# Half of a block product by seven multiplications instead of eight, in a full matmul stream

## The chip, the cores and the metric

One core of a Trainium2 chip. The metric is device microseconds of one execution: the median of three runs of the kernel before is 2508.51 us (2507.36 to 2508.7). The profile is of one more execution, of 2515.92 us, whose span from the first to the last instruction is 2513.9 us.

## The reference

One layer of a hybrid decoder on x of 2048 tokens by 1024 channels, all in float32:

```
h     = rms_norm(x)
proj  = h @ w_in                         # 1024 -> 8716 columns, split into
        u_a, z_a, q, k, v, z_b, xbc, dt, z_c, gate_logits (3 x 1024)
y_a   = s5_mixer(u_a) * silu(z_a)        # diagonal state space model, 512 wide
y_b   = attention(q, k, v) * silu(z_b)   # three dilated windows
y_c   = ssd_mixer(conv(xbc), dt, z_c)    # chunks of 128 tokens, gated norm
g     = sigmoid(gate_logits)
out   = x + (g0*(y_a@proj_a) + g1*(y_b@proj_b) + g2*(y_c@proj_c)) @ w_out
```

## The kernel before

Every product of two float32 matrices is three matmuls: both operands are split into a high part (float32r, written by ACT) and a low part (the rest, by DVE), and hi*hi, lo*hi and hi*lo are summed in PSUM. `ch_unit` (L384 to L394) does that for an output tile of 128 channels by 512 tokens: 8 steps of the contraction (k) by 3, so 24 matmuls of 512 columns.

The input projection takes the tokens in two halves of two blocks of 512 (`tb`). In the first half the columns come in the order q, k, v, z_b, dt and z_c, xbc (with its convolution), u and z, gates; in the second u and z come first. For the gates (`main_gates`, L555) twelve weight tiles of 256 columns come in one after the other, each as one load of 1 MB (`wload`, L353) into the one buffer `wr`, split in four pieces into `wh` and `wl` (L368, L369; six buffers each), and serve four output tiles, which ACT turns into tanh (L571) and SP stores to `g_d`.

A generator yields after each output tile (a unit). Beside the units runs background work: `run` (in `main`) gives it a number of steps between two units. In the first half these are the S5 tables and attention (units 41 to 80), then `ssd(0)` (83 to 135), `a0_early` (86 to 122: norm and transposes of the second half's rows of x, kept in DRAM as `hT_d`) and `out_weights` (88 to 134: the last stage's weights split in hi and lo, kept in DRAM as `pw_d` and `wo_d`). In the second half it is `s5` (153 to 180), `s5_glu` (181 to 196), attention and the start of `ssd(1)`.

A scheduler then lists the instructions of every engine in one fixed order, by its own model of when each becomes ready, and each engine runs its list in that order. SP issues all DMAs. PSUM has three banks for output tiles (`mm`) and five for the background (`c`).

Of the kernel before, what the change touches and what calls it, by code (L numbers as in the profile page):

```python
# [19 lines left out]
S = 2048  # L20
# [10 lines left out]
S5END = 196  # L31
# [118 lines left out]
class Hybrid:  # L150
# [4 lines left out]
    def setup(self, ctx):  # L155
# [29 lines left out]
        self.tab_d = dram("tab_d", [P, 8, 4 * TABW])  # L185
# [6 lines left out]
        self.wo_d = dram("wo_d", [4, P, 2, 8, 256])  # L192

# [57 lines left out]
    def ct(self, name, shape, dt=F32, tag=None, bufs=1):  # L251

        return self.jp.tile(list(shape), dt, name=name, tag=tag or name, bufs=bufs)

# [90 lines left out]

    def wload(self, name, specs):
# [57 lines left out]
    def main_qkv(self, half):  # L404
# [3 lines left out]
        for kind, g in units:  # L408
# [3 lines left out]
            for tb in (2 * half, 2 * half + 1):  # L412
                for pr in range(2):
# [11 lines left out]
                    nc.sync.dma_start(self.out_rows(dst, tb, pr), e)  # L425
# [21 lines left out]
    def main_uz(self, half):  # L447
        nc = self.nc
        for u in range(4):
            wt = self.wtile(f"uz{u}_{half}", [(u * 256, 256)])  # L450
            for tb in (2 * half, 2 * half + 1):
                for m in range(2):
# [16 lines left out]
                    nc.sync.dma_start(dst[r0:r0 + P, :, tb * 64:(tb + 1) * 64], e)  # L469
# [21 lines left out]
    def conv(self, ct, tb, ps):  # L491
# [3 lines left out]
        xb = self.gp.tile([P, 515], F32, name=f"xb_{nm}", tag="xb", bufs=3)  # L495
# [30 lines left out]
        nc.sync.dma_start(d[t0:t0 + 512, c0:c0 + P].rearrange("(i p) c -> p i c", p=P), yt)  # L526

    def main_dtz(self, half):
# [13 lines left out]
        for u in range(1, 3):  # L542
            wt = self.wtile(f"zc{u}_{half}", [(C_ZC + u * 256, 256)])
            for tb in (2 * half, 2 * half + 1):
                for pr in range(2):
# [6 lines left out]
                    nc.sync.dma_start(self.out_rows(self.zc_d, tb, pr)[:, :, u * 256:(u + 1) * 256], e)  # L552
                    yield

    def main_gates(self, half):  # L555
        nc = self.nc
        for u in range(12):
# [4 lines left out]
            for i, (m, tb) in enumerate(order):  # L562
                nm = f"g{u}_{m}_{tb}"
                if u == 11 and i == 2 and half == 0:
                    self.a0_late(2)
                elif u == 11 and i == 2:
                    self.ysplit = [self.load_y(0)]
# [126 lines left out]
    def merge(self):  # L694

        nc = self.nc
        for tt in range(16):
            rows = slice(tt * P, (tt + 1) * P)
            o = self.mp.tile([P, 3, 4, 66], F32, name=f"mo{tt}", tag="mo", bufs=2)
            for g in range(3):  # L700
                nc.sync.dma_start(o[:, g], self.o_d[g][rows])
            zb = self.mp.tile([P, 4, 64], F32, name=f"mz{tt}", tag="mz", bufs=1)
            nc.sync.dma_start(zb, self.zb_d[rows].rearrange("t (h d) -> t h d", d=64))
            sc = self.mp.tile([P, 3, 3, 4], F32, name=f"msc{tt}", tag="msc", bufs=2)
            w, wl, mx, den = sc[:, 0], sc[:, 1], sc[:, 2, 0, :], sc[:, 2, 1, :]
            nc.vector.tensor_max(mx, o[:, 0, :, 65], o[:, 1, :, 65])
            nc.vector.tensor_max(mx, mx, o[:, 2, :, 65])
            nc.vector.tensor_sub(w, o[:, :, :, 65], mx.unsqueeze(1).to_broadcast([P, 3, 4]))
            nc.scalar.activation(w, w, AF.Exp)
            nc.vector.tensor_mul(wl, w, o[:, :, :, 64])  # L710
# [4 lines left out]
            y = self.mp.tile([P, 4, 64], F32, name=f"my{tt}", tag="my", bufs=1)  # L715
            t = self.mp.tile([P, 4, 64], F32, name=f"mt{tt}", tag="mt", bufs=1)
            for g in range(3):
                wb = w[:, g].unsqueeze(2).to_broadcast([P, 4, 64])
                nc.vector.tensor_mul(t if g else y, o[:, g, :, 0:64], wb)
                if g:  # L720
                    nc.vector.tensor_add(y, y, t)
# [4 lines left out]
            yt = self.mp.tile([P, 2, P], F32, name=f"myt{tt}", tag="myt", bufs=1)  # L726
# [40 lines left out]
    def ssd(self, half):  # L767
        nc = self.nc
        for ch in range(half * 8, half * 8 + 8):
            yield from self.ssd_chunk(ch, slice((ch % 8) * 12, (ch % 8) * 12 + 12))  # L770

    def ssd_chunk(self, ch, hs):
# [703 lines left out]
```

## Time and profile before

| | before |
|---|---|
| median of three runs | 2508.51 us |
| profiled execution | 2515.92 us, span 2513.9 us |
| granted TensorE clock, mean | 0.989 |
| PE busy | 2450.5 us (97%) |
| DVE / ACT / POOL busy | 1325.0 / 782.5 / 700.4 us |
| HBM read / written | 304.80 / 145.97 MB |

The page puts 6% of the chain that ended last on each of the three matmul lines of the gates (`ps_g`, L392 to L394). A matmul's busy time runs from its start to its modelled end, and neighbours overlap; how fast a stream goes is read from one start to the next.

### The profile page before, as it was taken

How to read it: one execution, taken by the hardware profiler on the slowest of the kernel's cores; microseconds unless marked ns; L12 is line 12 of the kernel's file. 1: busy time of each engine (PE TensorE's matmuls, PEld its weight loads, DVE VectorE, ACT ScalarE, POOL GpSimd, SP SyncE). 2: the span in 40 equal slices, each digit the busy share in tenths (PEclk: the TensorE clock that was granted, in tenths of full speed). 3: DMA queues.
4: the chain of work that ended last, by engine and by line, in shares of the span. 5: the costliest groups of instructions: out<-in, count | busy, mean ns of one | idle time of the engine just before them, and what ended most of it. 6: DMA issues, size and time to landing. Idle time of an engine off the chain costs nothing.

```text
span 2513.9 us, 40157 instructions
## 1 busy us (share of the span) xinstructions
PE 2450.5 (97%) x15216; PEld 2155.8 (86%) x15216; DVE 1325.0 (53%) x2852; ACT 782.5 (31%) x1656; POOL 700.4 (28%) x737
## 2 busy tenths in 40 slices
PE   8999999999999999999999999999999899999999
PEld 8999988778888888899999988888888678888988
DVE  6963667853544333277765545632334767563321
ACT  4222235443443324222244244533332312121100
POOL 2262243501434430054342000000111455432120
PEclk8999999999999999999999999999999999999999
DMA  6443344447995336455554432433333688887986
GB/s 162 117 147 117 127 134 132 139 135 213 324 340 183 127 100 212 125 160 172 155 171 153 127 107 85 151 122 126 112 126 113 227 294 298 302 293 261 315 291 217
DMA packets 417088, 453.41 MB, mean 180 GB/s; under 512 B 103040, under 2 KB 358272, under 8 KB 409728
## 3 DMA queue, kind: packets, MB, share of 16 engines
q1 hardware_dynamic: 416896, 450.86, 56.2%
q8 instruction: 120, 1.97, 0.3%
q14 instruction: 72, 0.59, 0.1%
HBM read 304.80 MB, written 145.97 MB: 179 GB/s over the span
## 4 chain that ended last, share of the span: by engine, by line
PE 76%; DMA 8%; DVE 8%; POOL 4%; SPq 2%; issue 1%; ACT 1%; DVEq 0%; ACTq 0%; POOLq 0%
PE ps_g L392 6%; PE ps_g L394 6%; PE ps_g L393 6%; PE fp L1299 3%; PE fp L1301 3%; PE fp L1300 3%; PE ao L688 3%; PE ps_xbc L393 2%; PE ps_xbc L394 2%; PE ps_xbc L392 2%; PE ps_uz L394 2%; PE ps_uz L392 2%; PE ps_uz L393 2%; PE op L1332 2%; PE op L1330 2%; PE op L1331 2%
## 5 line engine op out<-in xcount | busy, mean ns | idle before, releaser
L392 PE MATMUL ps_g<-hT_hi,wh_g 128*128 128x512 f32 x768 | 308.4, 402 | 0.6 <-DVE e_uz L466 0.6
L394 PE MATMUL ps_g<-hT_hi,wl_g 128*128 128x512 f32 x768 | 306.4, 399 | 0.0
L393 PE MATMUL ps_g<-hT_lo,wh_g 128*128 128x512 f32 x768 | 305.7, 398 | 0.0
L813 POOL TENSOR_TENSOR sr<-tle,ahl 128x384 fp32r<-128x384 f32 x128 | 119.9, 960 | 447.3 <-PE sd L818 343.2
L392 PEld LDWEIGHTS ps_g<-hT_hi,wh_g 128*128 128x128 f32 x768 | 144.3, 188 | 33.3 <-DVE e_uz L466 1.3
L394 PEld LDWEIGHTS ps_g<-hT_hi,wl_g 128*128 128x128 f32 x768 | 144.5, 188 | 32.8
L393 PEld LDWEIGHTS ps_g<-hT_lo,wh_g 128*128 128x128 f32 x768 | 144.4, 188 | 32.4
L1299 PE MATMUL fp<-fy_hi,fp 128*128 128x512 f32 x384 | 153.9, 401 | 1.8 <-DMA fp<-pw_d 1.3
L1332 PE MATMUL op<-fo,fm_lo 128*128 128x256 f32 x512 | 146.6, 288 | 7.2 <-DVE fm_lo L1312 7.2
L1330 PE MATMUL op<-fo,fm_hi 128*128 128x256 f32 x512 | 148.0, 289 | 4.0 <-DMA fo<-wo_d 2.8
L1301 PE MATMUL fp<-fy_hi,fp 128*128 128x512 f32 x384 | 150.9, 393 | 0.0
L1300 PE MATMUL fp<-fy_lo,fp 128*128 128x512 f32 x384 | 150.3, 391 | 0.0
L1331 PE MATMUL op<-fo,fm_hi 128*128 128x256 f32 x512 | 146.3, 286 | 0.0
L1304 POOL TENSOR_TENSOR fm<-fm,fg 128x512 f32<-128x512 f32 x64 | 85.0, 1328 | 204.4 <-DVE fg L1302 193.7
L667 ACT ACTIVATE sm<-sm,ml 128x256 f32<-128x256 f32 (+1 forms) x192 | 86.4, 451 | 154.4 <-DVE ml L665 127.0
L392 PE MATMUL ps_xbc<-hT_hi,wh_xbc 128*128 128x512 f32 x320 | 129.7, 405 | 0.0
L394 PE MATMUL ps_xbc<-hT_hi,wl_xbc 128*128 128x512 f32 x320 | 129.4, 404 | 0.0
L393 PE MATMUL ps_xbc<-hT_lo,wh_xbc 128*128 128x512 f32 x320 | 129.1, 404 | 0.0
L369 DVE TENSOR_TENSOR wl_g<-wr_g,wh_g 128x512 fp32r<-128x512 f32 x96 | 75.1, 804 | 98.5 <-ACT wh_g L368 93.5
L506 DVE SCALAR_TENSOR_TENSOR ac_cv<-xb_cv,convw,ac_cv 128x512 f32<-128x512 f32 x120 | 101.3, 844 | 38.8 <-ACT ac_cv L504 38.5
L381 PE MATMUL ps_q<-wh_q,hT_hi 128*128 128x256 f32 x384 | 112.2, 293 | 2.1 <-ACT hT_hi L324 1.7
L382 PE MATMUL ps_q<-wl_q,hT_hi 128*128 128x256 f32 x384 | 110.8, 289 | 3.4 <-DVE wl_q L369 3.4
(418 smaller groups left out, 6922.7 us busy)
## 6 DMA issues: line engine op xcount, KB each, us to landing
fp<-pw_d SPq DMA_DIRECT2D x32, 1536.0 KB, 6.9
fo<-wo_d SPq DMA_DIRECT2D x16, 2048.0 KB, 8.7
wr_g<-in_w_in_dram SPq DMA_DIRECT2D x24, 1024.0 KB, 5.4
g_d<-e_g SPq DMA_DIRECT2D x96, 256.0 KB, 2.7
fg<-g_d SPq DMA_DIRECT2D x96, 256.0 KB, 7.4
pw_d<-owh SPq DMA_DIRECT2D x24, 512.0 KB, 7.1
wr_xbc<-in_w_in_dram SPq DMA_DIRECT2D x10, 1024.0 KB, 5.5
x<-in_x_dram SPq DMA_DIRECT2D x32, 256.0 KB, 5.4
```

The lines of the kernel that those rows point to most:

```text
L381: nc.tensor.matmul(ps, hi[:, t], wh, start=kt == 0, stop=False)
L382: nc.tensor.matmul(ps, hi[:, t], wl, start=False, stop=False)
L392: nc.tensor.matmul(ps, wh, hi, start=kt == 0, stop=False)
L393: nc.tensor.matmul(ps, wh, lo, start=False, stop=False)
L394: nc.tensor.matmul(ps, wl, hi, start=False, stop=kt == KT - 1)
L813: nc.gpsimd.tensor_mul(r, self.tle.unsqueeze(1).to_broadcast([P, 3, P]), ahl[:, i, h0:h0 + 3].unsqueeze(2).to_broadcast([P, 3, P]))
L1299: nc.tensor.matmul(ps, W[k][0], yh[k], start=k == k0, stop=False)
L1300: nc.tensor.matmul(ps, W[k][0], yl[k], start=False, stop=False)
L1301: nc.tensor.matmul(ps, W[k][1], yh[k], start=False, stop=k == k1 - 1)
L1330: nc.tensor.matmul(ps, mh[k][:, t], W[k][0], start=k == 0, stop=False)
L1331: nc.tensor.matmul(ps, mh[k][:, t], W[k][1], start=False, stop=False)
L1332: nc.tensor.matmul(ps, mlo[k][:, t], W[k][0], start=False, stop=k == 7)
```

## The change

The gates of the first half are one product of a 3072 x 1024 by a 1024 x 1024 matrix. The changed kernel does it per weight tile as a 2 x 2 block product after Strassen (in Winograd's form): seven products instead of eight, each of 12 matmuls (4 steps of k by 3). Blocks of h are t0 and t1 (the two token blocks) by the two halves of k. The names: products 1 to 7; `S` 1 to 4 are sums of blocks of h, made once; `gt` 1 to 4 are differences of the weight blocks `gr`, made per tile; `gx`, `gz`, `gq` hold copies of partial results.

```diff
+    def sums(self, half):
...
+            for nm, (hi, lo) in (("11", t0[k]), ("12", t0[4 + k]), ("21", t1[k]), ("22", t1[4 + k])):
+                a[nm] = self.ev(f"a{nm}_{half}_{k}")
+                v.tensor_add(a[nm], hi.bitcast(F32), lo.bitcast(F32))
...
+            v.tensor_add(s1, a["21"], a["22"])
+            v.tensor_sub(s2, s1, a["11"])
+            v.tensor_sub(s3, a["11"], a["21"])
+            v.tensor_sub(s4, a["12"], s2)
+            nc.sync.dma_start(self.sum_d[0, k], s2)
+            nc.sync.dma_start(self.sum_d[1, k], s4)
+            for i, x in ((1, s1), (3, s3)):
+                self.split(x, S[i][0][:, k, :], S[i][1][:, k, :])
...
+        hi = self.wp.tile([P, KT, 268], F32R, name=f"S2_{half}_hi", tag="wr", bufs=1)
...
+    def gate_ops(self, u):
...
+        b11, b12, b22, b21 = raw(0, 0), raw(0, 1), raw(1, 1), raw(1, 0)
+        yield put(1, b11)
+        t1 = diff(1, b12, b11)
+        yield put(5, t1)
+        t2 = diff(2, b22, t1)
+        yield put(6, t2)
+        yield put(3, b22)
+        t3 = diff(3, b22, b12)
+        yield put(2, b21)
+        t4 = diff(4, b21, t2)
+        yield put(7, t3)
+        yield put(4, t4)
...
+            for k, (hi, lo) in enumerate(opnd[p]):
+                wh, wl = w[0][:, k, :], w[1][:, k, :]
+                nc.tensor.matmul(ps, wh, hi, start=k == 0 and p in (1, 2, 5), stop=False, skip_group_check=True)
+                nc.tensor.matmul(ps, wh, lo, start=False, stop=False, skip_group_check=True)
+                nc.tensor.matmul(ps, wl, hi, start=False, stop=k == 3 and p in (2, 3, 4), skip_group_check=True)
+            if p == 1:
+                keep(u, f"x{u % 2}", ps)
+            elif p == 5:
+                keep(u, f"z{u % 2}", ps)
+            elif p == 6:
+                keep(u, "q", ps)
+            elif p == 4:
+                d = self.ev(f"g21_{nm}")
+                put(u, 1, 0, ps, d)
+            else:
+                d, b, m = {3: (e.get("q"), 0, 1), 2: (e.get(f"x{u % 2}"), 0, 0), 7: (e.get(f"z{u % 2}"), 1, 1)}[p]
+                nc.vector.tensor_add(d, d, ps)
+                put(u, b, m, d, d)
```

`put` of the products splits a weight block (ACT high, DVE low); `keep` is an ACT copy from PSUM; the last `put` is tanh and store. The second half's gates stay as they were. To make room in SBUF and on the engines, other work moves:

```diff
-        run([(self.s5_setup(), 18, 2, 38)], 40)
+        ssd0, early0 = self.ssd(0), self.a0_early()
+        run([(self.s5_setup(), 18, 2, 38), (early(early0, 5), 5, 20, 40)], 40)
...
-        run([(chain(self.attention(0, 0), self.attention(1, 0)), 40, 41, 80), (self.s5_tables(), 40, 41, 80),
-             (self.ssd_dt(0, self.jp), 3, 73, 80)], 82)
+        run([(chain(self.attention(0, 0), self.attention(1, 0)), 40, 41, 79), (early(tabs, 54), 54, 41, 80),
+             (self.ssd_dt(0, self.jp), 3, 73, 79), (early0, 3, 40, 52)], 80)
...
-        run([(ssd0, 64, 83, 135), (early0, 8, 86, 122), (self.out_weights(), 20, 88, 134)], 136)
+        sums = self.sums(0)
+        run([(tabs, 10, 80, 86), (early(sums, 4), 4, 81, 85)], 85)
+        run([(tabs, 10, 80, 86), (sums, 5, 85, 88)], 88)
...
+        run([(ssd0, 65, 89, 135)], 136)
...
-        run([(self.s5(), 42, 153, 180)], 180)
+        run([(self.s5(), 42, 153, 180), (early(ow, 13), 13, 138, 180)], 180)
...
-        run([(self.s5_glu(), 25, 181, S5END)], S5END)
+        run([(self.s5_glu(), 25, 181, 196), (ow, 7, 180, 196), (self.ssd_dt(1, self.jp), 2, 196, 198)], S5END)
```

The S5 tables come in 16 pieces of half the size instead of 8; `out_weights` in 40 pieces of 512 columns instead of 20 of 1024, with one buffer each; the first half's ssd has two buffers of `sr` and `smm` instead of four and three, one of `sb`, `sbt`, `sct` and `sz` instead of two, and loads its next chunk a step earlier; `merge` is rewritten for smaller tiles; `main_uz` loads its next weight tile a unit after the last instead of at its own start.

On DVE, at the last u and z units and the first gates, the order before is (`e_uz` the last u and z tiles, `sm` and `sx` ssd, `owh` the weight split, `wl_g` the low part of gate weights):

```order
L466 SCALAR_TENSOR_TENSOR e_uz_0_1_7229<-t_uz_0_1_7230,ps_uz_0_1_7204 128x64x8
L821 TENSOR_TENSOR sm_9_7241<-sm_9_7241,sgm_7023 128x384
L466 SCALAR_TENSOR_TENSOR e_uz_1_1_7280<-t_uz_1_1_7281,ps_uz_1_1_7255 128x64x8
L1240 SCALAR_TENSOR_TENSOR owh_8272<-ow_8270,snw,owh_8272 128x1024
L369 TENSOR_TENSOR wl_g_0_0_7553<-wr_g_0_7550,wh_g_0_0_7552 128x2x256
L369 TENSOR_TENSOR wl_g_0_1_7557<-wr_g_0_7550,wh_g_0_1_7556 128x2x256
```

Before, the low parts of the first gate tile stand ahead of these rows and those of the second right behind them. Now the same place reads (`S_0_lo` low parts of the sums of h, `sl` the sums read back from DRAM, `gt` and `wl_g` the operands of products 5 and 6 of the first tile):

```order
L483 SCALAR_TENSOR_TENSOR e_uz_1_0_7646<-t_uz_1_0_7647,ps_uz_1_0_7621 128x64x8
L616 TENSOR_TENSOR S_0_lo<-a_0_3_7567,S_0_hi 128x512
L616 TENSOR_TENSOR S_0_lo<-sl_0_0_7652,S_0_hi 128x512
L999 TENSOR_TENSOR sgm_7836<-sg_7833,tle 128x256
L616 TENSOR_TENSOR S_0_lo<-sl_0_1_7656,S_0_hi 128x512
L483 SCALAR_TENSOR_TENSOR e_uz_0_1_7693<-t_uz_0_1_7694,ps_uz_0_1_7668 128x64x8
L1018 TENSOR_TENSOR sm_0_7892<-sm_0_7892,sgm_7836 128x384
L616 TENSOR_TENSOR S_0_lo<-sl_0_2_7660,S_0_hi 128x512
L616 TENSOR_TENSOR S_0_lo<-sl_0_3_7664,S_0_hi 128x512
L483 SCALAR_TENSOR_TENSOR e_uz_1_1_7723<-t_uz_1_1_7724,ps_uz_1_1_7698 128x64x8
L642 TENSOR_TENSOR gt_1_7744<-gr_01_7734,gr_00_7732 128x512
L616 TENSOR_TENSOR wl_g_5_7747<-gt_1_7744,wh_g_5_7746 128x512
```

The sums of h stand between the last u and z tiles, and the first tile's operands from product 5 on come behind the last `e_uz`. On SP, where the second half's first weight tile is loaded (`wr_uz`), the order before is (`xl` the second half's h read back, `yc_d` an ssd result):

```order
L353 DMA wr_g_0_9825<-in_w_in_dram 128x8x256
L572 DMA g_d<-e_g_1_1_9601 128x512
L860 DMA yc_d<-sz_9294 128x6x128
L572 DMA g_d<-e_g_0_0_9667 128x512
L572 DMA g_d<-e_g_0_1_9712 128x512
L572 DMA g_d<-e_g_1_0_9767 128x512
L353 DMA wr_uz_1_10066<-in_w_in_dram 128x8x256
L572 DMA g_d<-e_g_1_1_9812 128x512
L572 DMA g_d<-e_g_0_0_9868 128x512
```

And now (`gr` raw weight blocks, `gq`, `gx`, `gz`, `g` finished gate tiles):

```order
L637 DMA gr_11_10097<-in_w_in_dram 128x4x128
L697 DMA g_d<-g_g_0_10078 128x512
L637 DMA gr_10_10099<-in_w_in_dram 128x4x128
L697 DMA g_d<-gq_0_10117 128x512
L697 DMA g_d<-gx_0_9789 128x512
L697 DMA g_d<-gz_0_10058 128x512
L973 DMA sct_10020<-cmT_d 128x2x128
L969 DMA sb_10016<-bm_d 128x256
L367 DMA wr_uz_1_10492<-in_w_in_dram 128x8x256
L348 DMA xl_0_10354<-hT_d 128x512
L697 DMA g_d<-g_g_0_10331 128x512
```

The load now has six of the first half's gate stores behind it, before it had five. Its buffer `wr` now holds the high part of sum 2 until product 6 of the last tile; before, it was free as soon as the last gate tile was split.

## Rows read from the trace of the kernel before

**Rows 1.** The page: span; busy us, share, count by engine.

```profile
span 2513.9 us, 40157 instructions
PE 2450.5 (97%) x15216; PEld 2155.8 (86%) x15216; DVE 1325.0 (53%) x2852; ACT 782.5 (31%) x1656; POOL 700.4 (28%) x737
```

**Rows 2.** Busy time by stretch: engines, granted clock, DMA share, rate.

```profile
core 0: us, PE busy (x) PEld busy (x) DVE busy (x) ACT busy (x) POOL busy (x), PEclk, DMA share, GB/s
0.00:200.00 200.00, 186.92 (x1472) 184.26 (x1473) 146.47 (x557) 66.61 (x129) 81.52 (x96) 0.94 0.52 142
585.00:760.00 175.00, 174.36 (x832) 143.47 (x832) 87.38 (x107) 73.52 (x128) 65.25 (x66) 1.00 1.02 321
639.70:972.20 332.50, 331.86 (x1590) 272.45 (x1589) 144.07 (x190) 118.09 (x229) 127.15 (x137) 1.00 0.64 206
1061.00:1200.00 139.00, 133.51 (x1015) 129.26 (x1013) 103.11 (x195) 35.69 (x69) 67.01 (x91) 1.00 0.58 167
1061.00:1420.00 359.00, 345.32 (x2719) 337.20 (x2718) 238.77 (x395) 116.82 (x209) 128.65 (x150) 1.00 0.53 156
1989.40:1996.20 6.80, 4.90 (x14) 3.72 (x15) 6.74 (x14) 0.74 (x3) 1.23 (x3) 0.50 1.05 439
```

**Rows 3.** Timeline of PE among the gates, twenty matmuls apart: start, length.

```profile
703.13 0.39 PE L394 MATMUL ps_g<-hT_hi,wl_g 128*128 128x512 f32 x1
...
707.76 0.40 PE L393 MATMUL ps_g<-hT_lo,wh_g 128*128 128x512 f32 x1
```

**Rows 4.** DVE groups in the gates: count | busy us, mean ns | idle before.

```profile
L369 DVE TENSOR_TENSOR wl_g<-wr_g,wh_g 128x512 fp32r<-128x512 f32 x44 | 38.9, 905 | 30.0 <-ACT wh_g L368 29.9
...
L1240 DVE SCALAR_TENSOR_TENSOR owh<-ow,owh 128x1024 fp32r<-128x1024 f32 x8 | 10.1, 1258 | 12.8 <-ACT owh L1239 12.8
L1240 DVE SCALAR_TENSOR_TENSOR owh<-ow,snw,owh 128x1024 fp32r<-128x1024 f32 x6 | 8.4, 1393 | 7.0 <-ACT owh L1239 7.0
...
L289 DVE TENSOR_SCALAR x<-x,xs 128x512 f32<-128x512 f32 x16 | 7.1, 484 | 7.6 <-POOL xs L246 7.6
```

**Rows 5.** POOL groups of the same stretch, 639.7 to 972.2 us.

```profile
L813 POOL TENSOR_TENSOR sr<-tle,ahl 128x384 fp32r<-128x384 f32 x54 | 49.6, 941 | 104.8 <-PE sd L818 104.8
...
L795 POOL TENSOR_TENSOR sx<-sx,hpar 128x768 f32<-128x768 f32 x7 | 13.8, 1965 | 0.4
...
L797 POOL TENSOR_TENSOR sxdd<-sxd,edc 128x768 f32<-128x768 f32 x7 | 11.5, 1637 | 0.0
L794 POOL TENSOR_TENSOR sxd<-sx,dt 128x768 f32<-128x768 f32 x7 | 10.3, 1474 | 25.7 <-PE syd L827 25.7
```

**Rows 6.** Single DVE and ACT instructions by tile: ns least, median, most.

```profile
L369 DVE TENSOR_TENSOR wl_g<-wr_g,wh_g x96: 675/692/1850, 628.4 to 1957.2; 128x512 fp32r<-128x512 f32 x96
...
L466 DVE SCALAR_TENSOR_TENSOR e_uz<-t_uz,ps_uz x16: 1047/1082/1096, 601.1 to 1062.0; 128x512 f32<-128x512 f32 x16
...
L721 DVE TENSOR_TENSOR my<-my,mt x32: 411/425/1411, 1931.0 to 2254.2; 128x256 f32<-128x256 f32 x32
...
L1082 DVE SCALAR_TENSOR_TENSOR s5ks<-ident,s5dd,s5ks x32: 216/217/223, 274.9 to 566.0; 16x16 f32<-16x16 f32 x32
...
L821 DVE TENSOR_TENSOR sm<-sm,sgm x64: 539/1074/1643, 610.5 to 2288.7; 128x384 f32<-128x384 f32 x64
...
L368 ACT CAST wh_g<-wr_g x96: 603/620/666, 627.7 to 1955.9; 128x512 fp32r<-128x512 f32 x96
...
L465 ACT ACTIVATE t_uz<-ps_uz x16: 587/598/632, 600.3 to 1061.4; 128x512 f32<-128x512 f32 x16
```

**Rows 7.** Waits of PE, 1061 to 1420: waiter, releaser, total, times, longest.

```profile
PE s5yp L1166 <- POOL s5r L1163: 6.8, 6, 2.1
```

**Rows 8.** Waits of PE from 1980 to 2000.

```profile
PE syd L827 <- DVE sm L821: 6.4, 2, 5.8
```

**Rows 9.** DMA issues by line: count, size, median us to landing.

```profile
wr_g<-in_w_in_dram SPq DMA_DIRECT2D x24, 1024.0 KB, 5.4
...
wr_uz<-in_w_in_dram SPq DMA_DIRECT2D x8, 1024.0 KB, 6.1
```

More of the change, by code (lines that the diff above doesn't have):

```diff
@@ L30 @@
 ATTEND = 256
-S5END = 196
+S5END = 198
 class Small:
@@ L253, in ct, with tct @@
         return self.jp.tile(list(shape), dt, name=name, tag=tag or name, bufs=bufs)
+    def tct(self, name, shape, dt=F32, tag=None, bufs=1):
+        return self.tp.tile(list(shape), dt, name=name, tag=tag or name, bufs=bufs)
     def sct(self, name, shape, dt=F32, tag=None, bufs=1):
@@ L448, in main_uz, with weights @@
         nc = self.nc
+        def weights(u):
+            return self.wtile(f"uz{u}_{half}", [(u * 256, 256)]) if u < 4 else None
+        nxt = weights(0)
         for u in range(4):
-            wt = self.wtile(f"uz{u}_{half}", [(u * 256, 256)])
+            wt, nxt = nxt, None
             for tb in (2 * half, 2 * half + 1):
@@ new lines, in split, with load_sum, pinned, raw @@
+    def split(self, x, hi, lo):
+        self.nc.scalar.copy(hi, x)
+        self.nc.vector.tensor_sub(lo, x, hi.bitcast(F32))
+    def load_sum(self, half, i, k, hi, lo):
+        e = self.ev(f"sl{half}_{i}_{k}")
+        self.nc.sync.dma_start(e, self.sum_d[i, k])
+        self.split(e, hi, lo)
+    def pinned(self, out, in_):
+        with self.tc.issue_after(self.anchor):
+            self.nc.sync.dma_start(out, in_)
+    def gate_ops(self, u):
+        nc = self.nc
+        w = self.A["w_in"][0].rearrange("(k p) c -> p k c", p=P)
+        def raw(i, j):
+            t = self.gp.tile([P, 528], F32, name=f"gr{u}_{i}{j}", tag="xb", bufs=3)
+            t = t[:, 0:512].rearrange("p (k c) -> p k c", c=P)
+            c0 = C_G + u * 256 + j * P
+            nc.sync.dma_start(t, w[:, i * 4:i * 4 + 4, c0:c0 + P])
+            return t
+        def diff(i, a, b):
+            t = self.ev(f"gt{u}_{i}", (P, 4, P))
+            nc.vector.tensor_sub(t, a, b)
+            return t
+        def put(p, x):
+            hl = []
+            for y in ("wh", "wl"):
+                t = self.wp.tile([P, 2, 268], F32R, name=f"{y}_g{u}_{p}", tag=y, bufs=6)
+                hl.append(t.rearrange("p k c -> p (k c)")[:, 0:512].rearrange("p (k c) -> p k c", c=P))
+            self.split(x, *hl)
+            return hl
+        b11, b12, b22, b21 = raw(0, 0), raw(0, 1), raw(1, 1), raw(1, 0)
[10 more added lines that the diff above has]
+        yield put(4, t4)
@@ L556, in main_gates, with main_gates_plain @@
+    def main_gates_plain(self, half):
         nc = self.nc
@@ L1418, in main @@
         st, self.jp = open_pool("jp3")
-        ssd, merge = chain(self.ssd_dt(1, self.sp), self.ssd(1)), self.merge()
+        ssd, merge = self.ssd(1), self.merge()
         run([(chain(self.attention(0, 1), self.attention(1, 1), self.attention(2, 1)), 72, S5END + 2, ATTEND),
-             (early(ssd, 12), 12, 236, ATTEND)], ATTEND)
+             (early(ssd, 11), 11, 236, ATTEND)], ATTEND)
         st.close()
```

282 lines of the change are left out of this document (187 added, 95 removed).

## The prediction

> **What bounds the kernel now.** I read the page first. PE is busy for 97% of the span [rows 1], but neighbouring matmuls overlap in that count, so the reader should go on to the table of stretches: from 639.7 to 972.2 us, where the first half's gates run, PE is idle for 0.6 of 332.5 us at a full clock (1.00, 2.4 GHz), while DVE works 144.1 and POOL 127.2 us [rows 2]. There the kernel is bound by the number of matmuls. It isn't everywhere: from 0 to 200 us PE lacks 13.1 us with DVE busy for 146.5, and from 1061 to 1200 it lacks 5.5 of 139 us with DVE busy for 103.1, 74% [rows 2]. So two questions decide. What does a matmul cost in the full stream, and does the added work push DVE into the state in which PE waits?
>
> **What is removed.** In the timeline, twenty gate matmuls start between 703.13 and 707.76 us [rows 3]: 4.63 / 20 = 0.2315 us each, well under the 0.39 us that one is shown as busy. Before, the first half's gates are 12 tiles x 4 units x 24 = 1152 matmuls; now 12 x 7 products x 12 = 1008 of the same shape. 144 x 0.2315 = 33.3 us go, and since PE has no gaps there, all of it is on the path. The transposes of `a0_early` only move.
>
> **The seam into the gates.** Product 1 uses blocks that exist, product 5 needs all of sum 1 and weights made after the last u and z unit. On DVE, 60 instructions stand between the first `e_uz` of the last eight units and the last one: 45 full tiles of the sums and splits and 2 of `wl_uz` at the 0.692 us of `wl_g` = 32.5 us; six `e_uz` at 1.082 = 6.5; three adds or masks of 256 columns at 0.425, four small table rows at 0.217, one `sm` at 0.539 = 2.7 [rows 6]. That is 41.7 us. PE gives it seven units of 24 x 0.2315 = 38.9 us and twelve small background matmuls (at half the pitch, my estimate, 1.4 us), from which 1.1 us fall away because the first `e_uz` itself takes 1.082: 39.2 us. DVE comes out 2.5 us late even when nothing else happens. POOL meanwhile makes two `sr`, `sxd`, `sx` and `sxdd` of the first ssd chunk, 1.9 + 1.5 + 2.0 + 1.6 = 7.0 us [rows 5], and DVE's own rows show what that does: `wl_g` takes 0.692 in the median and up to 1.850, `sm` 0.539 at the least and 1.074 in the median [rows 6]. So the delay is between 2.5 and 9.5 us; I take the middle, 6. From the last unit's end the chain is tanh 0.598, `e_uz` 1.082, `gt_1` 0.692, cast 0.620, `wl_5` 0.692 = 3.7 us [rows 6]; product 1 and the two matmuls of product 5 that want no low weight cover 14 x 0.2315 = 3.2. PE waits 0.5 us and the delay, 6.5 us. Behind a wait of 5.8 us [rows 8] the clock stood at 0.50, so 1.2 GHz, for 6.8 us [rows 2], which is 3.4 us of work lost; not every wait shows that, so I count half. Seam: 8 us, between 1 and 13.
>
> On this the Trainium skill (SBUF — State Buffer, "Who interferes with whom") has a rule against the change: a DVE instruction with two inputs in SBUF and a GpSimd instruction that reads SBUF exclude each other for their whole length, while DVE with one input in PSUM is left alone. The rows agree in kind: `e_uz`, which reads PSUM, stays within 1.047 to 1.096 us, and `wl_g` and `sm` spread to 1.850 and 1.643 [rows 6]. By the rule in full the delay is 9.5 and the seam 12 us; without it 2.5 and 5.
>
> **The gates themselves.** From DVE's 144.1 us [rows 2] go `wl_g` 38.9, the weight split 10.1 + 8.4 and the rows of x 7.1 [rows 4]; 79.6 remain. Each tile adds 7 splits and 4 differences, so 132 at the 0.905 us that `wl_g` takes beside the ssd [rows 4] = 119.5, and 36 adds from PSUM at no more than 0.692 = 24.9. Sum 224 us in 332.5 - 33.3 us, less the 64 transposes that move away (128 columns, each between a quarter and the whole of 0.2315: 4 to 15 us), so about 290 us: 77%. The stretch before that comes nearest, 1061 to 1200, has 74% and loses 4 us in 100 [rows 2], which would be 11.5 us. But 6.8 us of PE's waits there and a little after are one chain through POOL (`s5r`) [rows 7]; here the weights are made some four products ahead, 4 x 12 x 0.2315 = 11 us, against a cast and a split of 1.3 us and a raw load of at most 5.4 us [rows 6, 9]. I take 5, between 0 and 12. The shorter buffers of ssd are in it.
>
> **The seam out of the gates.** `wr` comes free with product 6 of the last tile. PE then has four more products, 11.1 us, and some 25 small ones of ssd (half the pitch, an estimate: 3 us). The load takes 6.1 us [rows 9], the first cast 0.62, and then DVE goes through some twelve rows of 0.7 to 0.75 us until the fifth step of the new h is there: 6.5 + 0.6 + 8.9 = 16.0 us. PE wants it at 14 + 12 x 0.2315 = 16.9. Just in time alone; each blocked row delays it. 3 us, between 0 and 7.
>
> **The moved work.** *Weight split*, 40 half pieces of about 0.63 us on DVE (1.258 / 2 [rows 4]), 25 us over units 138 to 198, 972 to about 1420 us. Before, it was hidden in the gates, so leaving there gives nothing. In its new place DVE works 238.8 of 359 us and PE lacks 13.7 [rows 2]. If the loss grows with DVE's load it is about 1 us; if a piece stands in front of an awaited link each time, some 16 pieces there cost 10. I take 3. Its transfers (20 tiles of 0.5 MB read, twice that written, 31.5 MB over 448 us) add 70 GB/s to 156; 321 GB/s from 585 to 760 us cost PE 0.6 us [rows 2], so I charge nothing for them. *Rows of x*, into the first 360 us: 7.1 us of DVE [rows 4] where 13.1 us are lost per 146.5 of DVE [rows 2] is 0.6; each of eight tiles held up once by its two scalings (0.97) is 8. I take 2, from -2 to 8, since the finer S5 tables beside them could also ease a wait. *ssd* loading a chunk earlier, the new `merge` and the earlier u and z loads: no wait of PE at u and z is there to be removed; at the end a wait like the 5.8 us for `sm` [rows 8] could go or come: 0, from -6 to 6.
>
> **Sum.** -33.3 + 8 + 5 + 3 + 3 + 2 = -12.3. The profiled execution took 2515.9 us (2.0 outside its span), so 2503.6; that is 7.4 above the median of the three runs, hence 2508.5 - 12.3 = 2496.2. I say 2496.
>
> **The rivals.**
> *All of it comes through.* The seams and the moved work stay near their lower ends, 5 us in all: 2508.5 - 33.3 + 5 = 2480. For it: DVE has slack on both sides of the first seam, and the stream of matmuls has held through 175 us with 1.02 of DMA [rows 2]. Against it: DVE's list at the seam is longer than PE's time even unblocked.
> *The gain is given back.* Every term near its upper half: 11 + 8 + 5 + 6 + 3 = 33: 2508. For it: wherever DVE is above 70%, PE lacks 4 to 7 in 100 us [rows 2]. Against it: the gates' lookahead.
> *DVE sets the pace in the gates.* Per tile PE takes 290 / 12 = 24.2 us. DVE takes 11 x 0.692 + 3 x 0.692 = 9.7 and 79.6 / 12 = 6.6 for the rest, 16.3; if it stood still for as long as POOL works, 127.2 / 12 = 10.6 [rows 2], 26.9. Only 3 raw buffers serve 4 raw blocks, so a tile's first load starts behind the tile before's `gt_3`; with 5.4 us for the load and 0.6 for the cast against five rows of DVE in between (3.5), 2.5 more: 29.4. With half the blocking it is 24.1, just under PE. It decides from 24.2 + (33.3 - 16) / 12 = 25.6 us per tile on; at 26.9 the gates alone give back 32 us and the other terms 16 more: 2508.5 - 33.3 + 32 + 16 = 2523. For it: the skewed `wl_g` and `sm`. Against: an `sm` and a mask of the rest read PSUM or wait for PE, and POOL's 127 us hold its own blocking too.
> The SBUF page's rule in the Trainium skill is this rival's mechanism; by it in full the tile would stand at 26.9 us, and the spread of `wl_g` [rows 6] bears it out only for some of the instructions.
>
> **How the numbers follow.** 0.45 for the forecast, 0.17 for 2480, 0.21 for the gain given back, 0.17 for the slower case. The medians of this kernel can be told apart by about 0.2%, 5 us: below 2503.5 is faster, above 2513.5 slower. The forecast's own terms reach from 2484 to 2507, nearly all faster: 0.43 + 0.17 = 0.60. The middle holds the case given back and the forecast's upper edge, 0.21; slower 0.19. The range, 2478 to 2515, leaves out the larger part of the slower case and a little below.
>
> **What would show it.** Right: 1008 gate matmuls in the first half, the same 0.23 us pitch, the gates some 290 to 300 us long, a wait of PE of 3 to 10 us between product 1 and the rest of product 5, DVE at three quarters there. Wrong: PE waiting in every tile for `wl_g` or for the adds from PSUM; or waits growing by more than 10 us between 1061 and 1420 or in the first 360 us; or no wait at the first seam. If the pitch were above 0.24 with no waits, the price of a matmul was wrong.

## The result and the profile after

The changed kernel takes 2528.18 us in the median of four runs (2526.05 to 2530.08), the kernel before, beside it, 2507.94: a ratio of 1.0083, 95% interval 1.0066 to 1.0101. It is slower by 0.8%, 20.2 us, where 2496 us was forecast. The profiled execution has a span of 2524.8 us, 10.9 more than that of the kernel before, which was taken in an execution 7.4 us above its median. So the profiles show about half of the loss.

The page of the changed kernel; answers to [rows 1]:

```profile
span 2524.8 us, 40656 instructions
PE 2435.3 (96%) x15072; PEld 2134.1 (85%) x15072; DVE 1439.3 (57%) x3104; ACT 835.9 (33%) x1780; POOL 718.9 (28%) x785
```

PE has its 144 matmuls fewer and 15 us less work, and the span is longer. To find the place I cut both traces at the same events, the first or last matmul of a group of columns (starts in us from each timeline of PE):

| stretch | before | after | change |
|---|---|---|---|
| front: to the last u and z matmul of the first half | 639.7 | 649.5 | +9.8 |
| gates of the first half, u and z of the second | 421.5 | 387.1 | -34.4 |
| second half's first q to last z_c matmul ("s5's stretch") | 411.7 | 440.8 | +29.1 |
| xbc | 165.6 | 163.8 | -1.8 |
| second half's gates | 345.3 | 350.3 | +5.0 |
| last stage, to the last matmul (4 us before the span's end in both) | 526.1 | 529.3 | +3.2 |

The gain arrives where it was forecast, and s5's stretch gives nearly all of it back. The front and the last stage of the kernel before may be long in this one execution: e2 and e10 below, which leave its last stage as it was, took 520.7 and 518.3 us for it, so its growth can be 9 to 11 us rather than 3. Stretches of after, with the columns of [rows 2], which they answer to (the gates, u and z, s5's stretch):

```profile
649.50:939.00 289.50, 287.46 (x1357) 234.74 (x1356) 197.66 (x270) 128.67 (x240) 127.54 (x118) 1.00 0.45 135
...
939.00:1036.50 97.50, 96.94 (x429) 78.16 (x428) 36.28 (x51) 34.18 (x55) 6.60 (x9) 1.00 0.80 227
1036.50:1477.40 440.90, 408.12 (x3146) 396.28 (x3145) 282.83 (x509) 147.75 (x274) 130.26 (x154) 0.97 0.67 200
```

And s5's stretch before:

```profile
1061.00:1473.00 412.00, 398.32 (x3185) 389.25 (x3183) 266.74 (x486) 134.17 (x253) 132.31 (x154) 1.00 0.51 153
```

PE is idle there for 32.8 us where it was for 13.7, and works 9.8 us longer on 39 instructions fewer, at a clock of 0.97 where it was 1.00. DVE has only 16 us more. PE's waits from 1036 to 1480 us (answers to [rows 7]):

```profile
PE s5yp L1363 <- POOL s5r L1360: 17.5, 12, 4.3
PE ps_q L395 <- ACT wh_q L382: 3.2, 1, 3.2
PE s5gp L1412 <- DVE s5gl L1405: 2.8, 2, 2.3
```

The same wait as before, 6.8 us in six, is now 17.5 in twelve. The chain of waits through two of them (start, length, what; stretches of PE left out):

```profile
1064.38 0.59 ACT e_q L446
1064.98 0.12 SPq L439
1065.10 0.05 issue
1065.15 3.81 DMA ow<-in_proj_b_dram
1069.00 0.04 issue
1069.04 0.64 ACT owh L1437
1069.71 0.69 DVE owl L1438
1070.40 0.61 DVE ss_q L449
...
1089.62 6.85 DMA wr_v<-in_w_in_dram
1096.49 0.63 ACT wh_v L382
1097.15 0.69 DVE wl_v L383
1097.84 0.60 DVE s5h L1351
1098.54 0.40 issue
1098.94 0.42 DVE s5r L1357
1099.36 0.66 DVE owl L1438
1100.05 0.42 DVE s5rt L1358
1100.48 0.43 DVE s5rt L1359
1100.98 0.73 POOL s5r L1360
1101.75 1.22 PE s5yp L1363 x2
1102.97 0.21 PE ps_k L395
```

The reader is to see two things. A raw piece of the weight split (`ow`) is loaded, and 3.9 us later its cast (`owh`) stands at the head of ACT's list, its subtraction (`owl`) at that of DVE's, and `ss_q` of the q columns behind it. And a link of s5 (`s5h`) stands on DVE behind `wl_v`, whose weight tile SP has issued late: 53.0 us after the stretch's first matmul, where before it was 37.4. SP and ACT stood at the split themselves; some of SP's and ACT's waits in the stretch (ACT's at the casts add up to 85 us):

```profile
SPq L1445 <- ACT owh L1437: 44.8, 17, 5.3
```

```profile
ACT owh L1437 <- DMA ow<-in_proj_c_dram: 29.2, 7, 8.0
ACT owh L1437 <- DMA ow<-in_w_out_dram: 21.4, 10, 4.4
```

Behind some of the waits the clock falls. After the last chain above, from 1102 to 1108 us, the granted clock is 0.53, so 1.2 GHz for most of the time:

```profile
1102.00:1108.00 6.00, 6.00 (x28) 5.82 (x29) 3.90 (x7) 1.60 (x4) 3.63 (x5) 0.53 0.95 261
```

### The profile page after: what moved, and what is told of

It is laid out like the page before. It is cut to its first block, busy times and chain, and to the rows that moved or that the text cites. A ratio compares the mean times of both kernels' runs of the same rounds, so it can differ in the third digit from the quotient of the medians.

```text
span 2524.8 us, 40656 instructions
## 1 busy us (share of the span) xinstructions
PE 2435.3 (96%) x15072; PEld 2134.1 (85%) x15072; DVE 1439.3 (57%) x3104; ACT 835.9 (33%) x1780; POOL 718.9 (28%) x785
## 4 chain that ended last, share of the span: by engine, by line
PE 67%; DMA 14%; DVE 10%; SPq 3%; issue 3%; POOL 2%; ACT 2%; ACTq 0%; DVEq 0%; POOLq 0%
PE ps_g L407 3%; PE ps_g L406 3%; PE ps_g L408 3%; PE ao L871 3%; PE fp L1497 3%; PE fp L1499 3%; PE fp L1498 3%; PE ps_xbc L406 2%; PE ps_xbc L408 2%; PE ps_xbc L407 2%; PE as L842 2%; PE op L1530 2%; PE op L1528 2%; PE op L1529 2%; PE psx_g L719 2%
## 5 line engine op out<-in xcount | busy, mean ns | idle before, releaser
L408 PE MATMUL ps_g<-hT_hi,wl_g 128*128 128x512 f32 x384 | 154.7, 403 | 0.0
L406 PE MATMUL ps_g<-hT_hi,wh_g 128*128 128x512 f32 x384 | 154.2, 402 | 0.0
L407 PE MATMUL ps_g<-hT_lo,wh_g 128*128 128x512 f32 x384 | 153.5, 400 | 0.0
L397 PE MATMUL ps_q<-wh_q,hT_lo 128*128 128x256 f32 x384 | 110.3, 288 | 3.5 <-DVE hT_lo L331 3.5
L396 PE MATMUL ps_v<-wl_v,hT_hi 128*128 128x256 f32 x384 | 110.2, 288 | 2.1 <-DVE wl_v L383 2.1
L395 PE MATMUL ps_v<-wh_v,hT_hi 128*128 128x256 f32 x384 | 111.9, 293 | 0.0
L396 PE MATMUL ps_k<-wl_k,hT_hi 128*128 128x256 f32 x384 | 109.8, 287 | 1.2 <-DVE wl_k L383 1.2
```

The source lines that it names most:

```text
L395: nc.tensor.matmul(ps, hi[:, t], wh, start=kt == 0, stop=False)
L396: nc.tensor.matmul(ps, hi[:, t], wl, start=False, stop=False)
L406: nc.tensor.matmul(ps, wh, hi, start=kt == 0, stop=False)
L407: nc.tensor.matmul(ps, wh, lo, start=False, stop=False)
L408: nc.tensor.matmul(ps, wl, hi, start=False, stop=kt == KT - 1)
```

## The experiments

All against the changed kernel, unless said; "stretch" is s5's stretch, read from the one profiled execution of each run; a time is the median of its executions. Theory: the weight split costs what the stretch lost. Then: by what? Its rows on ACT and DVE (C), its traffic (B2), or the standing of engines with a fixed order at the links between its loads, casts and stores (A, B1).

**e1, the split moved out.** To units 202 to 250, beside xbc and attention.

```diff
-        run([(self.s5(), 42, 153, 180), (early(ow, 13), 13, 138, 180)], 180)
+        run([(self.s5(), 42, 153, 180)], 180)
...
-             (early(ssd, 11), 11, 236, ATTEND)], ATTEND)
+             (early(ssd, 11), 11, 236, ATTEND), (ow, 20, 202, 250)], ATTEND)
```

> The changed kernel with one thing moved: the weight split runs beside the second half's attention (units 202 to 250) instead of beside s5 and s5_glu (units 138 to 198). In the changed kernel the stretch from the second half's first q matmul to the last z_c matmul takes 440.9 us, before 412. Theory (the weight split in that place is what it costs): the stretch falls to 412 to 418 us and the time from 2528 to 2498 to 2508. Rival (the stretch lost its time to something else, the place of the second ssd's tables or the earlier u and z loads): the stretch stays above 430 us and the time above 2520.

Stretch 408.7 us; median 2512.63, ratio to before 1.0018 (1.0005 to 1.0031). The stretch's loss is the split's. The time missed its 2498 to 2508, for half of the loss comes back in the second half's gates, 365.6 us instead of 350.3, and 7 us more in the last stage, 536.5 instead of 529.3. The stretch in e1:

```profile
1032.80:1441.50 408.70, 396.91 (x3144) 388.14 (x3144) 263.28 (x476) 130.49 (x239) 131.87 (x154) 0.99 0.52 156
```

**e2, only the split moved, in the kernel before.** With the changed kernel's `out_weights`:

```diff
-        run([(ssd0, 64, 83, 135), (early0, 8, 86, 122), (self.out_weights(), 20, 88, 134)], 136)
+        run([(ssd0, 64, 83, 135), (early0, 8, 86, 122)], 136)
...
-        run([(self.s5(), 42, 153, 180)], 180)
+        run([(self.s5(), 42, 153, 180), (early(ow, 13), 13, 138, 180)], 180)
```

> The kernel before, without the block product, with only the weight split moved to units 138 to 196 in the changed kernel's form (pieces of 512 columns, one buffer each, loads held behind the stores of the units). Theory: the move alone costs what the stretch lost, so 2508 + 22 to 32 = 2530 to 2540 us, with the waits of s5's second product for POOL up from 6.8 to about 15 us. Rival (the loss needs the block product's other moves): 2506 to 2513 us.

Stretch 440.7 us against 411.7; 2535.31, ratio 1.0111 (1.0089 to 1.0133). The move with the new form costs 29 us there; the block product has no part in it.

**e3, e6: data moved, nothing computed.** e6 has `bufs=3` for the raw piece besides.

```diff
-                nc.scalar.activation(hl[0], raw, AF.Copy, scale=scale)
-                nc.vector.scalar_tensor_tensor(hl[1], raw, scale, hl[0].bitcast(F32),
-                                               op0=ALU.mult, op1=ALU.subtract)
+                hl = [raw, raw]
```

> The changed kernel in which the weight split only moves data: each raw piece is stored twice without the ACT cast and the DVE subtraction, so the last stage computes with unsplit weights. DMAs, their places and sizes stay. Theory A (ACT and DVE stand in their queues behind the split's own loads): the stretch of 440.9 us falls to 412 to 420 and the time to 2500 to 2510. Theory B (the split's traffic delays the weight tiles and s5's tables, or SP stands behind its stores): the stretch stays at 430 to 441 us and the time at 2518 to 2528.

> The third run (the split only moves data, no cast and no subtraction) with three buffers for the raw pieces where it had one; the bytes, the packets and the units stay. Theory B1 (SP issues all DMAs in one order and stands still at the split's stores until the raw piece has landed, and at its loads until the stores have left the one buffer; weight tiles and s5's tables behind them come late): with three buffers the stretch falls from 446 us to 425 or less and the time from 2526.5 to 2506 or less. Theory B2 (the traffic itself slows the others' transfers): the stretch stays at 438 to 446 us, the time at 2519 to 2527.

e3: stretch 446.3 us, 2526.52. e6: 429.4 us, 2507.43, with the same bytes. So ACT and DVE need not take part (theory A of e3 fell), and buffers matter: in e3 SP stood 80 us for loads at the split's stores and 40 us for stores at its loads, in e6 48 us and none. Neither theory's bound on e6's stretch was met; it stays 21 us above e1's.

**e4, e5: computed, nothing moved.** 40 casts and subtractions on a constant tile in the old place, the real split as in e1. In e4 nothing held them; they ran ahead, from 964 to 1033 us, so e4 says nothing on the stretch (415.3 us; 2522.09). e5 holds each behind a weight cast:

```diff
+                with self.tc.issue_after(self.acast):
+                    nc.scalar.activation(hl[0], raw, AF.Copy, scale=0.5)
+                nc.vector.scalar_tensor_tensor(hl[1], raw, 0.5, hl[0].bitcast(F32),
+                                               op0=ALU.mult, op1=ALU.subtract)
```

> The split moved to units 202 to 250 as in the first run, and in its old place (units 138 to 198) only the 40 ACT casts and 40 DVE subtractions, on a constant tile, without any DMA; their results are not used. Theory C (DVE and ACT have no room there for 25 and 20 us more): the stretch takes 430 us or more and the time 2518 or more. Theories A and B (it is the loads and stores): the stretch takes 412 to 420 us, the time within 6 us of the first run's.

> As the fourth run, whose casts and subtractions ran ahead of the stretch (964 to 1033 us) since nothing held them: now each cast stands behind the weight casts of its unit, so that the 40 casts and 40 subtractions (constant tile, no DMA, results not used) are spread over units 138 to 198. The real split runs in units 202 to 250. Theory C (no room on DVE and ACT): the stretch from the first q matmul of the second half to the last z_c matmul takes 430 us or more (the first run had 408.7). Theory B (it is the loads and stores): 408 to 417 us.

e5: stretch 409.2 us, 2512.45. The rows cost nothing there; C falls:

```profile
1028.00:1437.20 409.20, 396.23 (x3145) 387.87 (x3143) 282.04 (x505) 146.69 (x267) 135.13 (x154) 0.99 0.52 156
```

**e7, e8, e10: other places, another form.** e7: the split in units 199 to 222. e8: back in the first half's gates, the low part over the raw piece. e10: the kernel before, the split in its old units, in pieces of 512 columns with one buffer each, their loads held behind a store. The first two lines are the part in which e7 differs from e1, the next two are e8, the last two e10:

```diff
-(ow, 20, 202, 250)
+(ow, 20, 199, 222)
...
-        run([(ssd0, 65, 89, 135)], 136)
+        run([(ssd0, 65, 89, 135), (self.out_weights(), 20, 89, 134)], 136)
...
-            raw = self.ct(f"ow{j}", [P, D], tag="ow", bufs=2)
+                raw = self.jp.tile([P, 512], F32, name=f"ow{j}_{q}", tag="ow", bufs=1)
```

> The changed kernel with the weight split in units 199 to 222, beside the second half's xbc columns, where PE was at 163.9 of 163.9 us with DVE at 98.6 and the rate at 113 GB/s. The split adds some 31 MB over about 170 us, 185 GB/s, so about 300 GB/s. If PE's long units there hide it as the first run's xbc did at 184 GB/s: s5's stretch 406 to 412 us, xbc 163 to 167, gates 345 to 352, the time 2492 to 2504, faster than the kernel before. If the transfers at 300 GB/s hold up the weight tiles: xbc 170 us or more, the time 2508 to 2520.

> The changed kernel with the weight split back in the first half's gates (units 89 to 134), its low part written over the raw piece to fit. DVE would work some 223 of 290 us there, the rate would be about 245 GB/s. If the long units hide it: the gates stay at 288 to 293 us, s5's stretch at 406 to 412, the time 2494 to 2505. If DVE at 77% or the loads of the raw gate blocks make PE wait (the prediction's rival of DVE setting the pace): gates 300 us or more, the time 2508 or more.

> The kernel before, the weight split left where it was, in the first half's gates (units 88 to 134), and only its form changed to the changed kernel's: 40 pieces of 512 columns with one buffer each instead of 20 of 1024 with two. Bytes and place stay. Theory B1: the form alone makes SP, ACT and DVE stand still there, the gates go from 332 us to 350 to 390 and the time from 2508 to 2525 to 2565. Rival (place and traffic decide, the form does not): gates 330 to 336 us, the time 2505 to 2513.

e7: xbc 181.4 us instead of 163.8, 2514.37. e8: gates with u and z 444.9 instead of 387.1; 2550.19, ratio 1.0171 (1.0151 to 1.0191). e10: the same two 447.2 instead of 421.5; 2532.27, ratio 1.0111 (1.0097 to 1.0125). Each came out as the dearer of its two expectations. e10 is the plain one: same units, same bytes, same sums, 26 us. It isn't the form alone, though: in the kernel before ACT's casts run from 601 to 750 us, and seven of the twenty start ahead of the gates; in e10, whose loads are held behind a store of u and z, they run from 643 to 904. Form and hold were not separated. ACT's waits in e10 from 636 to 996 us:

```profile
ACT owh L1244 <- DMA ow<-in_proj_c_dram: 42.2, 10, 5.3
...
ACT owh L1244 <- DMA ow<-in_w_out_dram: 39.2, 12, 5.5
```

**e9, e13, e16, e17: attempts to mend the split in its place.** e9, e16 and e17 also draw all 40 pieces into units 138 to 180, where the changed kernel has 26 of them. e9: three raw buffers, loads two steps ahead, stores one behind. e13: one buffer, but cast, subtraction, stores and next load held behind the next unit's evacuation and store. e16: both; e17: e16 with four buffers. The core of e16:

```diff
+                with self.tc.issue_after(self.acta):
+                    nc.scalar.activation(hl[m][0], raw[m], AF.Copy, scale=sc[m])
+                with self.tc.issue_after(self.dvea):
+                    nc.vector.scalar_tensor_tensor(hl[m][1], raw[m], sc[m], hl[m][0].bitcast(F32),
```

> The changed kernel with the weight split in s5's units (138 to 180) and all its bytes, casts and subtractions, but drawn apart: three buffers for the raw pieces and two each for the halves, a piece is loaded two steps before its cast and stored one step after it. Theory B1 (what costs is that SP, ACT and DVE stand still in their orders at each link of a piece that has one buffer): the stretch falls from 440.9 us to 409 to 420, the time from 2528 to 2498 to 2510. Theory B2 (the traffic of 31 MB beside s5's): the stretch stays at 425 or more, the time at 2512 or more.

> The changed kernel's weight split in its own place (units 138 to 196), pieces of 512 columns, one buffer each; only the order differs: a piece's cast is held on ACT behind the evacuation of the next unit, its subtraction on DVE likewise, its stores and the next load on SP behind that unit's store. So the load has a unit's time (5 us or more) before ACT comes to the cast. Theory B1 (what costs is standing: casts, subtractions and stores stood in their orders right where the load was reckoned to land, 3 us after its issue, and everything behind them stood too): the stretch falls from 440.9 us to 409 to 420, the time from 2528 to 2497 to 2508. Theory B2 (the traffic): the stretch stays at 430 or more, the time at 2516 or more.

> The ninth run (units 138 to 180, three buffers for the raw pieces, two for each half) with the order held as in the thirteenth: a piece's load, cast with subtraction, and stores are held behind the evacuations and stores of units n, n + 2 and n + 3, so that a load has two units, about 12 us, before ACT comes to its cast. In the thirteenth run casts still stood 3 to 5 us behind their loads in half of the cases. Theory B1 (standing): the stretch falls from e9's 441 us to 412 to 424, the time to 2500 to 2512. Theory B2, or a cost of 40 pieces there that is neither standing nor traffic: 430 or more.

> The sixteenth run with four buffers for the raw pieces and for each half where it had three and two. There ACT stood 62 us at the casts, now not for the load but for the store of the piece two before to leave the buffer of the high half. With four buffers a buffer comes round two units after its store was issued. Theory B1 (standing, whatever it waits for): ACT's standing at the casts falls under 15 us, the stretch from 444.5 to 412 to 424, the time to 2500 to 2512. Rival (40 pieces there cost by the rows themselves, whoever waits): the stretch stays at 432 or more.

Stretches 441.1, 434.7, 444.5 and 435.5 us; medians 2524.21, 2521.03, 2526.42, 2519.6. All four missed what theory B1 said and fell into the range of its rival. In e9 the casts had moved up with the loads; in e16 they stood for the stores to free their buffers. ACT's waits in the stretch, e9 and then e16:

```profile
ACT owh L1438 <- DMA ow<-in_w_out_dram: 36.6, 11, 6.2
ACT owh L1438 <- DMA ow<-in_proj_c_dram: 28.4, 6, 9.6
```

```profile
ACT owh L1439 <- DMA pw_d<-owh: 32.0, 12, 9.8
ACT owh L1439 <- DMA wo_d<-owh: 30.1, 9, 8.7
```

The standing had changed its link. In e17 ACT's at the casts is down to 34 us, from 85 in the changed kernel, and the stretch gains only 5. So the sum of ACT's standing does not give the price.

**e14, e18: traffic, and both without links.** e14: the split as in e1, and in the old place 80 copies inside DRAM that nothing waits for. e18: e14's copies and e5's rows together.

```diff
+            for x in range(2):
+                self.pinned(self.scr_d[n, x].rearrange("t p c -> p t c"), src)
```

> The first run (the real split beside the second half's xbc and attention), and in the old place, units 138 to 196, 80 copies of 256 KB inside DRAM in rows of 512 bytes, two per piece, each held behind a unit's store on SP; no engine waits for them and SP waits for none. 21 MB read and 21 MB written, against 10.5 read and 21 written by the split. Theory B1 (standing): the stretch stays within 8 us of the first run's 408.7. Theory B2 (traffic): the stretch is 425 or more.

> The fifth and the fourteenth run in one: in units 138 to 198 both the 40 casts and 40 subtractions on a constant tile and the 80 copies inside DRAM, with nothing that waits from one to the other; the real split runs beside the second half's xbc and attention. The fifth had a stretch of 409.2 us, the fourteenth 412.3, the changed kernel, where the same rows and about the same bytes wait for each other, 440.9. Theory B1 (the links between them cost: each stands in a fixed order until the other is done): 410 to 418 us. Rival (rows and traffic together use up the room that each alone leaves): 428 us or more.

e14: stretch 412.3 us, 2521.64. e18: 410.5 us, 2522.67 (both carry the real split too, late). The stretch in e14 and then in e18:

```profile
1037.20:1449.50 412.30, 397.96 (x3145) 389.39 (x3143) 263.61 (x476) 130.78 (x239) 132.16 (x154) 0.99 0.66 194
```

```profile
1033.00:1443.60 410.60, 397.72 (x3145) 388.45 (x3144) 281.09 (x505) 145.79 (x267) 133.67 (x154) 0.99 0.66 195
```

Beside the changed kernel's row e18 has nearly the same DVE, ACT and POOL time, DMA share and rate, and is 30 us shorter. What it lacks is the links. This decides for the links against rows and traffic, with two reservations. Copies inside DRAM have to stand for transfers with SBUF. And e18's profiled execution, 2514.41 us, is 8.3 below its median (e5's is 6.7 below): the medians of e14 and e18 are 9 and 10 us above e1's, of which their stretches show 4 and 2, and where the rest falls is not shown. Even with all 8.3 us put into the stretch, e18 would have 419, 22 short of the changed kernel.

**e11, e12, e15: looking for a better version.** e11: e1 in 80 pieces of 256 columns. e12: e11 with the rows of x back in the first half's gates. e15: e1's place, units 200 to 255, in e13's held order. The first and the last pair of lines are the parts in which e11 and e15 differ from e1:

```diff
-(ow, 20, 202, 250)
+(ow, 82, 200, 254)
...
-        run([(ssd0, 65, 89, 135)], 136)
+        run([(ssd0, 65, 89, 135), (early0, 8, 89, 122)], 136)
...
-(ow, 20, 202, 250)
+(ow, 41, 200, 255)
```

> As the first run (the split beside the second half's xbc and attention), but in 80 pieces of 256 columns with two buffers each, a piece loaded one step before its cast and stored one step after, 1.5 pieces per unit over units 200 to 254, in the same 6 KB. In the first run the gates of the second half took 365 us, before 345. Theory B1: gates 345 to 356 us, the time 2494 to 2505, faster than before. Rival (the traffic costs there): gates 360 us or more, the time 2508 to 2516.

> The run just before with the rows of x for the second half (the eight tiles that the change moved into the first 360 us) back among the first half's gates, units 89 to 122. If the front's 9 us are the 64 transposes themselves and moving them only moves that: u and z end 7 to 9 us earlier, the gates take as much longer, the time stays within 3 us of the run just before. Rival (the rows cost waits in the front that the gates would hide): the time falls by 5 us or more. Second rival (the gates with more DVE rows and transposes lose their lead): the gates take 12 us or more longer and the time rises by 5 us or more.

> The first run's place (units 200 to 255) with the held order of the thirteenth run. In the first run the second half's gates took 365.5 us against 350 in the changed kernel, with the pieces crowded into its first 140 us. Theory B1: with the pieces spread and held the gates take 348 to 356 us and the time is 2493 to 2504, faster than before. Theory B2: gates 360 us or more, the time 2509 or more.

e11: gates 367.6 us, 2520.96. ACT's casts waited for a load 43 times and 88 us in all, in e1 25 times and 83 us; it lost. e12, beside e11: front 637.4 us (12.9 less), gates with u and z 410.0 (25.5 more), 2540.14: the second rival. e15: gates 351.1 us, stretch 408.3, 2491.69, ratio 0.9938 (0.9923 to 0.9954): faster than both kernels. Against e1 its gates are 14.5 us and its last stage 8 us shorter; why the last stage is, wasn't followed. The second half's gates in e1 and then in e15, the same pieces, crowded up to 1737 us and held, so spread up to 1829:

```profile
1604.80:1970.40 365.60, 356.60 (x1874) 284.95 (x1872) 143.63 (x434) 123.66 (x336) 31.67 (x33) 1.00 0.54 167
```

```profile
1605.50:1956.60 351.10, 349.44 (x1879) 284.70 (x1878) 150.08 (x448) 126.89 (x338) 32.70 (x35) 1.00 0.56 175
```

## Why the prediction was wrong

**The step that failed is the weight split**, priced at 3 us, 0 to 10, in the paragraph on the moved work. It cost 29 us (the stretch of after and of e2; gone in e1). The price went by DVE's load and by a piece of 0.63 us standing in front of a link. But a piece holds an engine for as long as it waits for its own load (the 17 waits of ACT shown above are 3.0 us each, 8.0 at most), not for as long as it works; and it does so on ACT, then on DVE, then on SP. "I charge nothing for its transfers" was right for the traffic, as far as copies inside DRAM show it (e14: 3.6 us), and wrong for the waiting at them. "Before, it was hidden in the gates" missed that it wasn't the place alone that hid it, but also pieces of twice the size with two buffers, whose loads could run ahead (e10: 26 us for form and hold in the same units). The prediction counted what is queued and did not ask what each queued row waits for.

**The matmuls, -33.3:** right. The pitch is the same as in [rows 3], twenty matmuls from one to the other of these two starts of after:

```profile
703.11 0.39 PE L718 MATMUL psx_g<-hT_lo,wh_g 128*128 128x512 f32 x1
...
707.74 0.39 PE L717 MATMUL psz_g<-hT_hi,wh_g 128*128 128x512 f32 x1
```

**The seams, 8 and 3, and the gates, 5:** too dear. PE's waits from 640 to 960 us:

```profile
PE ps_uz L406 <- DVE e_uz L483: 2.3, 1, 2.3
PE psz_g L717 <- ACT wh_g L615: 1.9, 1, 1.9
```

The cause was right, DVE's list behind the sums, and the sizes were not. Product 5 (`psz_g`) waits 1.9 us, where the text's sign was 3 to 10; the other 2.3 us stand at 644 us, ahead of the last u and z unit, so in the front. Together they are 4.2 instead of 6.5, and the clock stayed at 1.00 in the gates. Of the 34.4 us that gates, u and z gained, 33.3 are matmuls; the 64 transposes that left for the front are worth at most the 9.8 us by which that grew, if nothing else there got shorter. So at most some 9 us were lost in seams, gates, and u and z together, an estimate, 16 forecast. Two slips in the working change little: the rows that it lists on DVE at the first seam add up to 61, not 60, and the load of 6.1 us at the second enters as 6.5.

**DVE as the pace of the gates:** false here. A tile took some 289.6 / 12 = 24.1 us (at the end of the 289.6 us 12 of the 1008 matmuls were still to come), with DVE at 197.7 of 289.5 us, 68% where 77% was forecast. Mean times of DVE's rows in the gates (answers to [rows 4]):

```profile
L616 DVE TENSOR_TENSOR wl_g<-gt,wh_g 128x512 fp32r<-128x512 f32 x48 | 38.1, 807 | 6.3 <-ACT wh_g L615 6.3
L616 DVE TENSOR_TENSOR wl_g<-gr,wh_g 128x512 fp32r<-128x512 f32 x35 | 30.4, 869 | 7.7 <-ACT wh_g L615 7.4 <-PE psx_g L719 0.2
L642 DVE TENSOR_TENSOR gt<-gr,gt 128x512 f32<-128x512 f32 x24 | 21.8, 906 | 4.5 <-DMA gr<-in_w_in_dram 4.3
```

They still spread above the median of 0.692 us in [rows 6]. Single rows show with what: of these rows and the other `gt`, 131 in all, the 79 with no POOL instruction beside them took 0.675 to 0.693 us, the 52 with one up to 1.959. By this the Trainium skill's rule on who excludes whom (SBUF — State Buffer, "Who interferes with whom") is there in kind; its full price, 26.9 us a tile, did not come. But the gates are near an edge: with the split in one-buffer pieces (e8) or the rows of x (e12) in them they, with u and z, lost 58 and 26 us.

**Rows of x, 2 us, 8 at most:** the front grew by 9.8, or by 12.9 by e12. The prediction had their transposes, 4 to 15 us by its own bounds, moving at no net price, so what the rows alone cost beside them can't be read off. In the gates rows and transposes would have cost 25.5 (e12); the move pays.

**ssd, merge and u and z, 0:** xbc, the second half's gates and the last stage are 6.4 us longer together, just past the upper end of -6 to 6, and 12 to 14 if the last stage before is that of e2 and e10; 72 small matmuls that moved from s5's stretch and xbc into the second half's gates are in that.

With the split at 3 us the kernel would stand near 2528.2 - 26 = 2502 us; e15, which takes nearly all of it out, stands at 2491.69. The forecast, 2496, lies between. That e15 comes so near it is luck in part: seams and gates were some 7 us too dear, the front about as much too cheap. The text named its own failure, waits growing by more than 10 us between 1061 and 1420.

**What stays open:** why e17, with 34 us of standing left at the casts, keeps 24 us that e18 does not pay. Its links are fewer, not gone: of the chain of work that ended last, followed through the stretch, 50 of 435.5 us still are loads, rows and stores of the split, 83 of 440.8 in the changed kernel. Holding a row also puts it elsewhere among s5's rows, and 29 of its 40 casts fall in s5's 238 us at a DMA share of 0.83; this was not separated. Nor was a transfer with SBUF tried that nothing waits for; e6 comes nearest, with SP still standing 48 us, and its stretch is 21 us above e1's. So that the links cost is shown by e18; that it is by standing at the head of an engine's list is argued from the waits, and no version in this place made the loss go away. The same page of the Trainium skill (SBUF — State Buffer, "Who interferes with whom") gives DMAs ports of their own, by which they would not slow the engines' rows; the traces agree, s5's rows on DVE last as long in after (the first row), with the split's loads and stores beside them, as in e18, where the split's transfers were replaced by copies inside DRAM:

```profile
L1357 DVE TENSOR_TENSOR s5r<-s5w,s5h 128x256 f32<-128x256 f32 x32 | 13.6, 425 | 1.2
```

```profile
L1358 DVE TENSOR_TENSOR s5r<-s5w,s5h 128x256 f32<-128x256 f32 x32 | 13.6, 426 | 1.3
```

## What to carry to other kernels

Don't price a background row by how long it runs: ask what it waits for and what stands behind it while it waits. A load, a cast and a store with one buffer make ACT, DVE and SP stand in turn. When such work is moved, ask what hid it (the place, its buffers, the size of its pieces) and take all of that along. And where a scheduler puts a row right behind the reckoned end of its load, hold it behind a later event, in a stretch with room: in the second half's gates that gave 14.5 us (e15 against e1), in s5's stretch the held versions gained 6 at most (e13).

## What the hardware showed that I had not expected

40 GB/s more beside s5 (194 instead of 153) lengthened the stretch by only 3.6 us in e14 (412.3 against e1's 408.7), though transfers took longer: in e18's stretch the loads `s5u` take 4.7 us in the median against 2.5 before, `s5p` 5.3 against 3.2. A wait can cost more than its length: after the 4.3 us wait that ends at 1101.75 the 256-column matmuls start 0.21 us apart, where before the wait it was 0.12, for some 6 us; over the stretch that is 9.8 us of work beside 19.1 of idling.
